# A transformer block on one Trainium2 core: input products of the feed-forward sublayers by Strassen's algorithm

## The chip, the cores and the metric

The kernel runs on 1 core of one Trainium2 chip. The metric is the time of one execution on the device in microseconds (us); a profiled execution also gives a span, from its first to its last instruction. The engines of the core are TensorE (PE; its weight loads are PEld), VectorE (DVE), ScalarE (ACT) and GpSimd (POOL); SyncE (SP) issues all transfers here.

## The reference

One block of a hybrid network on 512 tokens of width 1024, in float32: a feed-forward sublayer, a mixer (pooling and a state-space scan) and a second feed-forward sublayer, each behind a normalisation that is scaled and shifted by values computed from a conditioning vector `c`, and a last normalisation. What the change touches are the two feed-forward sublayers:

```
def swiglu(h, w_in, w_out):
    a, b = jnp.split(h @ w_in, 2, axis=-1)
    return (jax.nn.silu(a) * b) @ w_out

mod = (jax.nn.silu(c) @ w_ada[layer] + b_ada[layer]).reshape(bsz, 3, 3, D_MODEL)
h = modulate(rmsnorm(x, norm_g[layer, 0]), shift[:, 0], scale[:, 0])
x = x + 0.5 * gate[:, 0, None, :] * swiglu(h, ffn1_in[layer], ffn1_out[layer])
```

`h` is 512 x 1024, `w_in` 1024 x 5632, `w_out` 2816 x 1024.

## The kernel before, in words

**Products.** Every tile has 128 partitions. Activations are kept transposed: 8 tiles `h[k]` of 128 features by 512 tokens. A float32 value is held as two float32r numbers, a rounded high part and the difference to it, the low part; a product is three matmuls, high by high, high by low, low by high (`mm3`, lines 306 to 314), each with a weight load of its own, summed in a PSUM bank over k. A bank holds 512 columns, and there are eight.

**Pairs.** The 22 tiles of hidden features go in pairs: tile a for the gate, tile b for the value (`pair`, line 610). Each is a `product` over k = 0 to 7 of 512 columns. `glu` (line 601) takes Silu of a on ScalarE (605), multiplies by b on VectorE (607) and splits the result into parts (`split`, line 322: cast on ScalarE, difference on VectorE).

**Portions.** `ffn` (line 617) makes the pairs of one portion (PORTIONS: 8, 8 and 6), then the output products of that portion: 8 tiles m, each a product over the portion's pairs, added to `x` by `add_out` (524). In the last portion all but two output tiles are made in halves of 256 tokens, so that the next normalisation can begin. The first three pairs of the first sublayer are made in the start (`first_pairs`), k by k as the tiles `h[k]` are normalised; the first two of the second are made in halves (`in_halves`).

**Weights.** The class `Weights` (line 85) streams units of up to 8 tiles (512 KB). `load` starts the transfer into one of RAW = 3 raw tiles; `ensure` splits a unit, cast on ScalarE (123) and difference on VectorE (126), into a ring of RING = 5; `fill`, called at each new unit, keeps splits AHEAD = 3 units in front and loads RAW units in front of those.

**Conditioning.** The rest of `w_ada` (112 tiles of 256 KB, `ada_rest`, line 427) is multiplied on VectorE in the background of the first sublayer: `pump(n)` makes n steps, each a load and a `scalar_tensor_tensor` (466) on two SBUF tiles. PUMPS = (6, 1): six behind each pair, one behind each output tile. PREADA = 5 loads run ahead.

**Order.** TensorE's instructions stand in the order of the code (`manual_schedule`). In the start this holds for every engine. After it the framework orders the queues of the other engines by when inputs are ready, earlier code first; on the chip each queue is then worked in its order. Long-lived tiles come from NBIG = 50 tiles of 512 columns ("big").

Of the kernel before, what the change touches and what calls it, by code (L numbers as in the profile page):

```python
# [20 lines left out]
PORTIONS = ((0, 8), (8, 16), (16, 22))  # L21
# [10 lines left out]
RAW = 3  # L32
AHEAD = 3
NBIG = 50
NSQ = 2
NTMP = 8
PREADA = 5
PUMPS = (6, 1)
# [46 lines left out]
class Weights:  # L85


    def __init__(self, nc, pool, units, big):
        self.nc, self.pool, self.units, self.big = nc, pool, units, big
        self.raw, self.split = [], []  # L90
        self.first, self.ring = [0], [0]
        for _, count, _, extra in units:
            self.first.append(self.first[-1] + count)
            self.ring.append(self.ring[-1] + (not extra))
        self.at = self.done = 0
        self.unit = -1
        self.auto = False

    def load(self, upto):
        while len(self.raw) < min(upto, len(self.units)):  # L100
            ap, count, width, _ = self.units[len(self.raw)]
            raw = self.pool.tile([P, KD * P], F32, name="w_raw", tag="w_raw", bufs=RAW)
            self.nc.sync.dma_start(out=raw[:, :count * width], in_=ap)
            self.raw.append(raw)

    def ensure(self, upto, between=None):
        nc = self.nc
        while len(self.split) < min(upto, len(self.units)):
# [3 lines left out]
            raw, self.raw[i] = self.raw[i], None  # L112
            parts = []
            step = NT if extra else KD * P
            for c in range(0, count * width, step):
                n = min(step, count * width - c)
                if extra:
# [10 lines left out]
            self.split.append(parts)  # L128

    def fill(self, more=0):  # L130
# [7 lines left out]
        self.load(min(self.unit + AHEAD + RAW + more, len(self.split) + RAW))  # L138
# [23 lines left out]
class Norm:  # L162


    def __init__(self, blk, sub):
        self.blk, self.sub, self.rs = blk, sub, {}
        self.h = [None] * KD

# [10 lines left out]
    def apply(self, sl, k):  # L179
        if self.h[k] is None:  # L180
            self.h[k] = self.blk.new_act()
        self.blk.modulate(self.sub, k, sl, self.rs[sl], self.h, k % 2 == 1)
# [55 lines left out]
class Block:  # L238
# [26 lines left out]
    def plan(self):  # L265
# [9 lines left out]
        def ffn(f, first):  # L275
            for pi, (p0, p1) in enumerate(PORTIONS):
                for t in range(2 * max(p0, first), 2 * p1):
                    u.append((a["ffn%d_in" % f][t], KD, P, False))
# [27 lines left out]
    def mm3(self, ps, w, act, sl, first, last):  # L306
# [5 lines left out]
        T.matmul(o, lhsT=hi, rhs=ahi[:, s], start=first, stop=False)  # L312
        T.matmul(o, lhsT=hi, rhs=alo[:, s], start=False, stop=False)  # L313
        T.matmul(o, lhsT=lo, rhs=ahi[:, s], start=False, stop=last)  # L314
# [186 lines left out]
    def modulate(self, sub, k, sl, rs, h, pool):  # L501
# [7 lines left out]
        if pool:  # L509
            nc.vector.tensor_tensor(out=t, in0=self.x[:, k, s], in1=rs, op=ALU.mult)  # L510
            h32 = self.tmp()[:, :n]
            nc.scalar.activation(out=h32, in_=t, func=AF.Identity, scale=gs, bias=shift)
            self.split(h32, hi, lo, sl, pool=True)
# [62 lines left out]
    def in_halves(self, n, norm, finish):  # L576

        ws = []
        for sl in (HALF_A, HALF_B):
# [18 lines left out]
            finish(pss, sl)  # L598

# [10 lines left out]
    def pair(self, h, g):  # L610
        pa = self.bank()
        self.product(pa, None, h)
        pb = self.bank("t")
        self.product(pb, None, h)
        self.glu(pa, pb, FULL, g)

    def ffn(self, h, gs, j, gate, norm, late, spread, pumps=(0, 0)):
# [24 lines left out]
    def first_pairs(self):  # L642
# [67 lines left out]

        def prepare(k):
            self.ada_turn(k, rows[k])
            self.modulate(0, k, FULL, rs, h, False)

# [20 lines left out]
        for k in range(KD):  # L735
# [18 lines left out]
            if k > 5:  # L754
                self.W.ensure(k + 4)
        self.W.auto = True
# [8 lines left out]
        return h, gs  # L765
# [322 lines left out]
    def run(self):  # L1088
        h, gs = self.start()
# [6 lines left out]
        self.ffn(h, gs, NSTART, 2, lambda: norm(1), LATE1, SPREAD1, PUMPS)  # L1096
# [7 lines left out]
        self.in_halves(4, norms[2], glu_halves)  # L1104
        final = Final(self, 0)
        self.ffn(norms[2].h, gs, 2, 8, lambda: final, LATE2, SPREAD3)
# [80 lines left out]
```

## Time and profile before

| | |
|---|---|
| median of 3 runs | 1160.99 us (1160.63 to 1163.83) |
| the profiled execution | 1160.53 us |
| its span | 1158.5 us |
| TensorE busy | 1146.2 us, 99% |
| VectorE busy | 629.9 us, 54% |
| ScalarE busy | 396.6 us, 34% |
| GpSimd busy | 119.3 us, 10% |
| read from memory | 137.08 MB |

Matmuls are pipelined: the profile gives a duration of about 0.4 us to one whose successor starts 0.23 us later, so the price of a matmul is the distance of two starts. Busy times are unions, so they don't count an overlap twice. Stages, from the starts of the timeline: start to 69 us, first feed-forward to 400, mixer to 767, second feed-forward to the end.

### The profile page before, as it was taken

What the parts mean: (1) busy time and instruction counts of PE and PEld (TensorE: products, weight loads), DVE (VectorE), ACT (ScalarE), POOL (GpSimd) and SP (SyncE); (2) the same over time, 40 slices, a digit from 0 to 9 for tenths busy, and PEclk for the clock granted to TensorE, in tenths of its full rate; (3) what the DMA queues carried; (4) which work ended last, traced back from release to release, by engine and by line L of the source; (5) the groups of instructions that cost most, each with busy time, mean ns of one, the idle gap of its engine ahead of it and who ended that gap; (6) DMA issues with size and microseconds to landing.
All of it is one profiled execution on the core that took longest, in us unless ns stands there. A gap on an engine that the chain in (4) does not pass through costs nothing.

```text
span 1158.5 us, 15066 instructions
## 1 busy us (share of the span) xinstructions
PE 1146.2 (99%) x5948; PEld 940.8 (81%) x5948; DVE 629.9 (54%) x975; ACT 396.6 (34%) x660; POOL 119.3 (10%) x122
## 2 busy tenths in 40 slices
PE   8999999999999999999999999999999999999997
PEld 6677787777877997888888878899888888888887
DVE  4567736667363666677968595563333333333334
ACT  4352222221223453454544453343321222212232
POOL 0000000000000320023112561121000000000001
PEclk9999999999999999999999999999999999999999
DMA  9585735756352411222212213440332233323312
GB/s 346 170 293 178 261 115 198 256 190 228 123 178 91 141 60 52 77 73 73 74 55 73 73 56 91 124 131 20 91 91 91 93 103 96 92 91 91 95 33 73
DMA packets 52837, 140.17 MB, mean 121 GB/s; under 512 B 7456, under 2 KB 8864, under 8 KB 52768
## 3 DMA queue, kind: packets, MB, share of 16 engines
q1 hardware_dynamic: 52768, 139.23, 37.1%
q8 instruction: 46, 0.75, 0.3%
q14 instruction: 23, 0.19, 0.1%
HBM read 137.08 MB, written 2.10 MB: 120 GB/s over the span
## 4 chain that ended last, share of the span: by engine, by line
PE 98%; DVE 1%; DMA 0%; ACT 0%; SPq 0%; issue 0%; DVEq 0%; ACTq 0%
PE ps_mm L312 24%; PE ps_mm L313 23%; PE ps_mm L314 23%; PE ps_t L314 6%; PE ps_t L313 6%; PE ps_t L312 6%; PE ps_y L965 1%; PE ps_mm L352 1%; PE ps_mm L406 1%; PE ps_t L959 1%; PE ps_y L984 1%; PE ps_mm L375 1%; PE ps_t L927 0%; DMA x<-in_x_dram 0%; PE ps_t L930 0%; PE ps_t L932 0%
## 5 line engine op out<-in xcount | busy, mean ns | idle before, releaser
L312 PE MATMUL ps_mm<-big,w_hi 128*128 128x512 f32 (+1 forms) x1192 | 454.9, 382 | 0.0
L313 PE MATMUL ps_mm<-big,w_hi 128*128 128x512 f32 (+1 forms) x1192 | 448.1, 376 | 0.1
L314 PE MATMUL ps_mm<-big,w_lo 128*128 128x512 f32 (+1 forms) x1192 | 448.0, 376 | 0.0
L123 ACT CAST w_hi<-w_raw 128x1024 fp32r<-128x1024 f32 (+1 forms) x178 | 185.9, 1045 | 521.3 <-PE ps_mm L313 309.4
L126 DVE TENSOR_TENSOR w_lo<-w_raw,w_hi 128x1024 fp32r<-128x1024 f32 (+1 forms) x178 | 220.8, 1242 | 171.7 <-ACT w_hi L123 160.6
L312 PEld LDWEIGHTS ps_mm<-big,w_hi 128*128 128x128 f32 x1192 | 224.1, 188 | 50.3 <-issue 8.2
L314 PEld LDWEIGHTS ps_mm<-big,w_lo 128*128 128x128 f32 x1192 | 224.1, 188 | 44.8
L313 PEld LDWEIGHTS ps_mm<-big,w_hi 128*128 128x128 f32 x1192 | 224.2, 188 | 43.6 <-issue 0.7
L314 PE MATMUL ps_t<-big,w_lo 128*128 128x512 f32 x312 | 123.4, 396 | 0.0
L312 PE MATMUL ps_t<-big,w_hi 128*128 128x512 f32 x312 | 123.4, 396 | 0.0
L313 PE MATMUL ps_t<-big,w_hi 128*128 128x512 f32 x312 | 123.4, 396 | 0.0
L524 DVE SCALAR_TENSOR_TENSOR x<-ps_mm,mod,x 128x512 f32<-128x512 f32 (+1 forms) x79 | 51.1, 648 | 127.6 <-PE ps_mm L314 127.5
L331 POOL TENSOR_TENSOR sacc<-sacc,sq 128x256 f32<-128x256 f32 (+1 forms) x30 | 28.7, 956 | 747.4 <-ACT sq L386 416.1
L607 DVE TENSOR_TENSOR tmp<-tmp,ps_t 128x512 f32<-128x512 f32 x39 | 26.8, 688 | 104.4 <-PE ps_t L314 104.4
L466 DVE SCALAR_TENSOR_TENSOR big<-big,sc 128x512 f32<-128x512 f32 x98 | 73.6, 751 | 12.6 <-DMA big<-in_ada_dram 10.1
L314 PEld LDWEIGHTS ps_t<-big,w_lo 128*128 128x128 f32 x312 | 58.6, 188 | 14.2
L313 PEld LDWEIGHTS ps_t<-big,w_hi 128*128 128x128 f32 x312 | 58.6, 188 | 14.2
L312 PEld LDWEIGHTS ps_t<-big,w_hi 128*128 128x128 f32 x312 | 58.6, 188 | 14.1
L877 DVE SCALAR_TENSOR_TENSOR big<-ps_mm,vec,big 128x511 f32<-128x511 f32 (+2 forms) x60 | 44.7, 745 | 2.2 <-ACT big L875 1.3
L325 ACT CAST big<-tmp 128x512 fp32r<-128x512 f32 (+1 forms) x66 | 36.5, 556 | 2.0 <-DVE tmp L607 1.4
L312 PE MATMUL ps_mm<-big 128*128 128x256 f32 x128 | 36.5, 286 | 0.0
L313 PE MATMUL ps_mm<-big 128*128 128x256 f32 x128 | 36.2, 283 | 0.0
(179 smaller groups left out, 891.1 us busy)
## 6 DMA issues: line engine op xcount, KB each, us to landing
w_raw<-in_ffn_in_dram SPq DMA_DIRECT2D x78, 512.0 KB, 3.5
big<-in_ada_dram SPq DMA_DIRECT2D x144, 256.0 KB, 4.8
w_raw<-in_ffn_out_dram SPq DMA_DIRECT2D x44, 512.0 KB, 3.8
w_raw<-in_w_in_dram SPq DMA_DIRECT2D x32, 512.0 KB, 3.5
w_raw<-in_w_outB_dram SPq DMA_DIRECT2D x10, 512.0 KB, 3.6
w_raw<-in_w1s_dram SPq DMA_DIRECT2D x8, 384.0 KB, 5.8
w_raw<-in_w_outA_dram SPq DMA_DIRECT2D x6, 512.0 KB, 3.9
x<-in_x_dram SPq DMA_DIRECT2D x8, 256.0 KB, 5.3
```

What stands on the lines that cost most here:

```text
L123: nc.scalar.copy(out=hi[:, :n], in_=r)
L126: nc.vector.tensor_tensor(out=lo[:, :n], in0=r, in1=hi[:, :n].bitcast(F32), op=ALU.subtract)
L312: T.matmul(o, lhsT=hi, rhs=ahi[:, s], start=first, stop=False)
L313: T.matmul(o, lhsT=hi, rhs=alo[:, s], start=False, stop=False)
L314: T.matmul(o, lhsT=lo, rhs=ahi[:, s], start=False, stop=last)
L325: self.nc.scalar.copy(out=hi[:, s], in_=src[:, :n])
L331: self.nc.gpsimd.tensor_tensor(out=acc, in0=acc, in1=q, op=ALU.add)
L352: self.nc.tensor.matmul(ps[:, at + j:at + j + 1], lhsT=acc[:, c * P - c0:(c + 1) * P - c0], rhs=self.ones[:, 0:1], start=i == 0, stop=i == ...
L466: V.scalar_tensor_tensor(out=acc, in0=ws.pop(i), scalar=self.sc[:, q:q + 1], in1=acc, op0=ALU.mult, op1=ALU.add)
L524: self.nc.vector.scalar_tensor_tensor(out=xs, in0=ps[:, :n], scalar=self.mod[:, gate, m:m + 1], in1=xs, op0=ALU.mult, op1=ALU.add)
L607: nc.vector.tensor_tensor(out=g32, in0=sa, in1=pb[:, :n], op=ALU.mult)
L877: V.scalar_tensor_tensor(out=acc[:, s:], in0=ps[:, :NT - s], scalar=tap(3 - s), in1=acc[:, s:], op0=ALU.mult, op1=ALU.add)
```

## The change

Input products of pairs 3 to 21 of the first sublayer and 2 to 21 of the second are made by the Winograd form of Strassen's algorithm. A pair is seen as a 2 x 2 block product: two halves of k, two weight tiles, two halves of the tokens. `quad` makes seven block products (4 values of k, three matmuls each of 256 columns) in three banks that it writes in turns, and takes sums out of them with copies on ScalarE and additions on VectorE. `combine` makes the sums of the activations (four new pairs of tiles per sublayer for each of two sums, `tq`), in the start and in `in_halves`. The sums of weights are made on GpSimd: three of 512 columns when a pair's two tiles are loaded (`sums`), one in front of the split of the last, half, unit. A pair now has three and a half units. The low part of a pair's result goes to GpSimd but for the last pair of a portion. There are four portions (7, 5, 4, 6), four raw tiles, three conditioning loads ahead instead of five, and PUMPS = (5, 3, 3): behind a pair of the first portion, a pair of the others, an output tile.

```
-PORTIONS = ((0, 8), (8, 16), (16, 22))
+PORTIONS = ((0, 7), (7, 12), (12, 16), (16, 22))
-RAW = 3
+RAW = 4
+NSUM = 2
+LOADS = 5
-NBIG = 50
+NBIG = 51
-PREADA = 5
-PUMPS = (6, 1)
+PREADA = 3
+PUMPS = (5, 3, 3)
...
+    def sums(self, a, b):
+        G = self.nc.gpsimd
+        t = self.pool.tile([P, 2, NT], F32, name="w_sum", tag="w_sum", bufs=NSUM)
+        a11, a12, a21, a22 = a[:, :NT], a[:, NT:], b[:, :NT], b[:, NT:]
+        G.tensor_tensor(out=t[:, 0], in0=a21, in1=a22, op=ALU.add)
+        G.tensor_tensor(out=t[:, 1], in0=t[:, 0], in1=a11, op=ALU.subtract)
+        G.tensor_tensor(out=a21, in0=a11, in1=a21, op=ALU.subtract)
+        return t
...
+            elif extra == 0.5:
+                if self.rawout + 2 > RAW or self.sumout + 1 > NSUM:
+                    return
+                self.rawout += 2
+                self.sumout += 1
+                a, b = self.raw_tile(ap[0]), self.raw_tile(ap[1])
+                t = self.sums(a, b)
+                self.raw += [a, t.rearrange("p c n -> p (c n)"), b, (a[:, NT:], t[:, 1])]
...
+            if extra == 3.5:
+                raw, second = raw
+                nc.gpsimd.tensor_tensor(out=raw, in0=raw, in1=second, op=ALU.subtract)
...
-        self.load(min(self.unit + AHEAD + RAW + more, len(self.split) + RAW))
+        self.load(min(self.unit + AHEAD + LOADS + more, len(self.split) + LOADS))
...
+    def combine(self, k, src):
+        G, V = self.nc.gpsimd, self.nc.vector
+        a, b = src[k], src[k + KD // 2]
+        la, lb = slice(*HALF_A), slice(*HALF_B)
+        t, u = self.tmp(), self.tmp()
+        V.tensor_tensor(out=t[:, la], in0=a[:, lb], in1=a[:, la], op=ALU.subtract)
+        V.tensor_tensor(out=t[:, lb], in0=b[:, lb], in1=t[:, la], op=ALU.subtract)
+        G.tensor_tensor(out=u[:, la], in0=b[:, lb], in1=a[:, lb], op=ALU.subtract)
+        G.tensor_tensor(out=u[:, lb], in0=b[:, la], in1=t[:, lb], op=ALU.subtract)
+        both = self.new_act(), self.new_act()
+        self.split(t, *both[0])
+        self.split(u, *both[1])
+        return both
+
+    def quad(self, h, tq):
+        V, S, W = self.nc.vector, self.nc.scalar, self.W
+        n = KD // 2
+        low, up = h[:n], h[n:]
+        t12, t34 = [t[0] for t in tq], [t[1] for t in tq]
+        def block(ps, ws, acts, sl, first):
+            for k in range(n):
+                self.mm3(ps, ws[k], acts[k], sl, first and k == 0, k == n - 1, True)
+        x, y, z = self.bank(), self.bank("t"), self.bank("y")
+        one, two = self.tmp(), self.tmp()
+        la, lb = slice(*HALF_A), slice(*HALF_B)
+        wa = W.take(2 * n, hold=True)
+        block(x, wa[:n], low, HALF_A, True)
+        S.copy(out=one[:, la], in_=x[:, la])
+        block(y, wa[n:], up, HALF_A, True)
+        V.tensor_tensor(out=one[:, la], in0=one[:, la], in1=y[:, la], op=ALU.add)
+        W.release(2 * n, False)
+        ws = W.take(2 * n, hold=True)
+        block(x, ws[n:], t12, HALF_B, False)
+        S.copy(out=one[:, lb], in_=x[:, la])
+        block(z, ws[:n], t12, HALF_A, True)
+        S.copy(out=two[:, lb], in_=z[:, la])
+        W.release(2 * n, False)
+        wb = W.take(2 * n, hold=True)
+        block(x, wb[:n], t34, HALF_A, False)
+        V.tensor_tensor(out=two[:, lb], in0=two[:, lb], in1=x[:, la], op=ALU.add)
+        block(z, W.take(n, hold=True), up, HALF_B, False)
+        V.tensor_tensor(out=one[:, lb], in0=one[:, lb], in1=z[:, la], op=ALU.add)
+        block(x, wb[n:], t34, HALF_B, False)
+        W.release(3 * n)
+        return one, two, x
+
+    def quad_pair(self, h, tq, g, pool):
+        V, S = self.nc.vector, self.nc.scalar
+        one, two, x = self.quad(h, tq)
+        la, lb = slice(*HALF_A), slice(*HALF_B)
+        S.activation(out=one, in_=one, func=AF.Silu)
+        V.tensor_tensor(out=two[:, lb], in0=one[:, lb], in1=two[:, lb], op=ALU.mult)
+        V.tensor_tensor(out=two[:, la], in0=one[:, la], in1=x[:, la], op=ALU.mult)
+        self.split(two, *g, pool=pool)
...
-                self.pair(h, gs[i])
-                self.pump(pumps[0])
+                self.quad_pair(h, tq, gs[i], i < p1 - 1)
+                self.pump(pumps[pi > 0])
+            if not pi:
+                self.pump(1)
+                self.pump(1)
...
-                self.pump(pumps[1])
+                self.pump(pumps[2])
...
+        def whole(k):
+            sums[k] = self.big()
+            nc.gpsimd.tensor_tensor(out=sums[k], in0=h[k][0].bitcast(F32), in1=h[k][1].bitcast(F32), op=ALU.add)
+            if k >= KD // 2:
+                tq.append(self.combine(k - KD // 2, sums))
```

In the second sublayer the normalised tile is also kept whole (`modulate` writes it to a tile of its own before the split, for every k), and `combine` runs after the first half of `in_halves`. `skip_group_check` in `mm3` and a smaller scratch area for transfers are the rest.

## Rows read from the trace of the kernel before

**Rows 1.** The page: busy time by engine; the chain that ended last

```profile
PE 1146.2 (99%) x5948; PEld 940.8 (81%) x5948; DVE 629.9 (54%) x975; ACT 396.6 (34%) x660; POOL 119.3 (10%) x122
...
PE 98%; DVE 1%; DMA 0%; ACT 0%; SPq 0%; issue 0%; DVEq 0%; ACTq 0%
```

**Rows 2.** Stretches (from:to): length, busy us (instructions) by engine, clock, DMA

```profile
core 0: us, PE busy (x) PEld busy (x) DVE busy (x) ACT busy (x) POOL busy (x), PEclk, DMA share, GB/s
0.00:69.48 69.48, 64.21 (x390) 47.91 (x391) 37.26 (x78) 29.81 (x49) 2.80 (x6) 0.98 0.74 255
...
172.50:259.70 87.20, 87.20 (x409) 68.00 (x407) 55.15 (x72) 24.78 (x36) 0.00 (x0) 1.00 0.61 210
...
752.60:767.00 14.40, 14.40 (x124) 14.40 (x122) 4.47 (x8) 3.90 (x6) 3.20 (x3) 1.00 0.37 128
...
917.26:1001.26 84.00, 84.00 (x361) 67.62 (x360) 27.42 (x29) 23.63 (x30) 0.00 (x0) 1.00 0.32 94
```

**Rows 3.** Timeline of TensorE, 512 columns: start, duration (us), line

```profile
150.09 0.40 PE L312 MATMUL ps_mm<-big,w_hi 128*128 128x512 f32 x1
...
157.09 0.40 PE L312 MATMUL ps_mm<-big,w_hi 128*128 128x512 f32 x1
```

**Rows 4.** Timeline of TensorE, 256 columns, 120 matmuls from first to last

```profile
752.59 0.28 PE L312 MATMUL ps_mm<-big,w_hi 128*128 128x256 f32 x1
...
766.67 0.28 PE L314 MATMUL ps_mm<-big,w_lo 128*128 128x256 f32 x1
```

**Rows 5.** Groups by line and shape, second feed-forward: count, busy us, mean ns

```profile
L126 DVE TENSOR_TENSOR w_lo<-w_raw,w_hi 128x1024 fp32r<-128x1024 f32 x56 | 68.6, 1225 | 82.8 <-ACT w_hi L123 78.3
...
L123 ACT CAST w_hi<-w_raw 128x1024 fp32r<-128x1024 f32 x57 | 60.1, 1055 | 233.9 <-PE ps_mm L313 148.5 <-issue 64.9 <-PE ps_t L313 16.2
...
L607 DVE TENSOR_TENSOR tmp<-tmp,ps_t 128x512 f32<-128x512 f32 x20 | 13.8, 689 | 71.2 <-PE ps_t L314 71.2
L327 DVE TENSOR_TENSOR big<-tmp,big 128x512 fp32r<-128x512 f32 x20 | 13.7, 685 | 0.0
...
L325 ACT CAST big<-tmp 128x512 fp32r<-128x512 f32 x20 | 12.5, 623 | 0.0
...
L327 DVE TENSOR_TENSOR big<-tmp,big 128x256 fp32r<-128x256 f32 x2 | 0.8, 426 | 0.1
L607 DVE TENSOR_TENSOR tmp<-tmp,ps_mm 128x256 f32<-128x256 f32 x2 | 0.8, 421 | 6.6 <-PE ps_mm L314 6.6
```

**Rows 6.** Groups of ScalarE by shape: a 256-column copy out of PSUM

```profile
L409 ACT COPY tmp<-ps_mm 128x256 f32<-128x256 f32 x8 | 3.0, 374 | 16.1 <-PE ps_mm L406 16.1
```

**Rows 7.** Line 987, GpSimd, two 512-column inputs: minimum, median, maximum ns

```profile
L987 POOL TENSOR_TENSOR big<-big x12: 1270/1298/2141, 493.0 to 696.5; 128x512 f32<-128x512 f32 x12
```

**Rows 8.** Groups of VectorE by shape: a conditioning step

```profile
L466 DVE SCALAR_TENSOR_TENSOR big<-big,sc 128x512 f32<-128x512 f32 x98 | 73.6, 751 | 12.6 <-DMA big<-in_ada_dram 10.1
```

**Rows 9.** Timeline of VectorE in the mixer

```profile
573.64 2.27 DVE L126 TENSOR_TENSOR w_lo<-w_raw,w_hi 128x1024 fp32r<-128x1024 f32 x1 [1.03 <-PE ps_t L961]
...
576.12 0.73 DVE L974 SCALAR_TENSOR_TENSOR big<-big,vec,ps_y 128x512 f32<-128x512 f32 x1
...
581.59 1.22 DVE L126 TENSOR_TENSOR w_lo<-w_raw,w_hi 128x1024 fp32r<-128x1024 f32 x1
...
664.08 1.01 DVE L342 TENSOR_TENSOR root<-root 128x4 f32<-128x4 f32 x1
```

**Rows 10.** Timeline of GpSimd at the same moments

```profile
573.55 1.27 POOL L987 TENSOR_TENSOR big<-big 128x512 f32<-128x512 f32 x1
...
576.02 1.33 POOL L331 TENSOR_TENSOR big<-big,sq 128x512 f32<-128x512 f32 x1
581.75 1.93 POOL L331 TENSOR_TENSOR big<-big,tmp 128x384 f32<-128x384 f32 x1 [4.40 <-DVE tmp L985]
...
664.04 1.04 POOL L778 TENSOR_TENSOR tmp<-tmp 128x510 f32<-128x510 f32 x1
```

**Rows 11.** The page, DMA issues: the conditioning loads

```profile
big<-in_ada_dram SPq DMA_DIRECT2D x144, 256.0 KB, 4.8
```

More of the change, by code (lines that the diff above doesn't have):

```diff
@@ L93, in __init__ @@
             self.first.append(self.first[-1] + count)
-            self.ring.append(self.ring[-1] + (not extra))
+            self.ring.append(self.ring[-1] + (extra is not True))
         self.at = self.done = 0
@@ L167, in __init__ @@
         self.h = [None] * KD
+        self.whole = [None] * KD
     def scale(self, k):
@@ L181, in apply, with combine @@
             self.h[k] = self.blk.new_act()
-        self.blk.modulate(self.sub, k, sl, self.rs[sl], self.h, k % 2 == 1)
+            if self.sub == 2:
+                self.whole[k] = self.blk.big()
+        self.blk.modulate(self.sub, k, sl, self.rs[sl], self.h, k % 2 == 1, self.whole[k])
+    def combine(self):
+        return [self.blk.combine(k, self.whole) for k in range(KD // 2)]
 class Final(Norm):
@@ L275, in ffn @@
         def ffn(f, first):
+            w = a["ffn%d_in" % f]
             for pi, (p0, p1) in enumerate(PORTIONS):
-                for t in range(2 * max(p0, first), 2 * p1):
-                    u.append((a["ffn%d_in" % f][t], KD, P, False))
+                for j in range(max(p0, first), p1):
+                    u.append(((w[2 * j], w[2 * j + 1]), KD, P, 0.5))
+                    u.extend((None, n, P, part) for n, part in ((KD, 1.5), (KD, 2.5), (KD // 2, 3.5)))
                 stream(a["ffn%d_out%d" % (f, pi)])
@@ L303, in mixer_order, with mm3 @@
                 + [("outB", m) for m in range(MLATE)])
-    def mm3(self, ps, w, act, sl, first, last):
+    def mm3(self, ps, w, act, sl, first, last, again=False):
         hi, lo = w
@@ L311, in mm3 @@
         T = self.nc.tensor
-        T.matmul(o, lhsT=hi, rhs=ahi[:, s], start=first, stop=False)
-        T.matmul(o, lhsT=hi, rhs=alo[:, s], start=False, stop=False)
-        T.matmul(o, lhsT=lo, rhs=ahi[:, s], start=False, stop=last)
+        T.matmul(o, lhsT=hi, rhs=ahi[:, s], start=first, stop=False, skip_group_check=again)
+        T.matmul(o, lhsT=hi, rhs=alo[:, s], start=False, stop=False, skip_group_check=again)
+        T.matmul(o, lhsT=lo, rhs=ahi[:, s], start=False, stop=last, skip_group_check=again)
     def product(self, ps, ws, acts, sl=FULL, mid=None):
@@ L498, in pump, with modulate @@
             next(self.bg, None)
-    def modulate(self, sub, k, sl, rs, h, pool):
+    def modulate(self, sub, k, sl, rs, h, pool, whole=None):
         nc = self.nc
@@ L598, in in_halves @@
             finish(pss, sl)
+            if sl == HALF_A and norm.sub == 2:
+                tq = norm.combine()
+        return tq
     def glu(self, pa, pb, sl, g):
@@ L608, in glu, with ffn @@
         self.split(g32, g[0], g[1], sl)
[L610 to L617, printed above, removed]
+    def ffn(self, h, tq, gs, j, gate, norm, late, spread, pumps=(0, 0, 0)):
         for pi, (p0, p1) in enumerate(PORTIONS):
@@ L713, in prepare @@
             self.modulate(0, k, FULL, rs, h, False)
+            if k > 1:
+                whole(k - 2)
         for k in range(3):
@@ L755, in first_pairs @@
                 self.W.ensure(k + 4)
+                whole(k)
         self.W.auto = True
@@ L1088, in run @@
     def run(self):
-        h, gs = self.start()
+        h, tq, gs = self.start()
         norms = {}
```

43 lines of the change are left out of this document (28 added, 15 removed).

## The prediction

> **What bounds the kernel now.** I read the page first: TensorE is busy 99% of the span and the chain that ended last is TensorE for 98%, so the sum of matmul times is the time [rows 1]. The table of stretches comes next. Over eight pairs of the first feed-forward TensorE never stops, VectorE works 55.2 of 87.2 us, GpSimd not at all; over 84 us of the second, VectorE works 27.4 [rows 2]. Third, the timeline of TensorE, since a busy matmul is no price: starts give it. From 150.09 to 157.09 us there are 30 steps of 512 columns, 0.2333 us each [rows 3]; from 752.59 to 766.67 us 119 steps of 256 columns, each with its own weight load, 0.1183 us each [rows 4]. Half the columns cost 0.507 of the time, though the weight loads are then busy for the whole stretch [rows 2]. That decides whether Strassen can pay at all.
>
> **What is removed.** The changed pairs are 3 to 21 of the first feed-forward and 2 to 21 of the second, 39. A pair is 2 x 8 x 3 = 48 matmuls of 512 columns, 48 x 0.2333 = 11.20 us [rows 3]. A quad is 7 blocks x 4 x 3 = 84 matmuls of 256, 84 x 0.1183 = 9.94 us [rows 4]. The gain is 1.26 us a pair, 49 us in all, if TensorE never waits.
>
> A rule speaks against this. The Trainium skill, TensorE: Matmul & The Clock Gate, section Back-to-back issue gap, gives a sustained stream with weight loads about 81 ns a matmul at 128 columns and 131 at 512; an estimate between them, 98 ns at 256, would make a quad 8.2 us against 6.3 for a pair, 31% longer instead of 11% shorter. The two timelines here show 118 and 233 ns, so I take the trace.
>
> **What is added, per quad.** Durations are from [rows 5] unless named.
> - VectorE: 3.5 units of weights instead of 2, three differences of 1.225 (line 126) and one of 512 columns, priced by the 512-column difference of line 327 (0.685): 4.36. Three adds and a multiply that read PSUM, 4 x 0.421 = 1.68. One multiply from two SBUF tiles, 0.43. Together 6.47 us; before it was 2 x 1.225 + 0.689 + 0.685 = 3.82.
> - ScalarE: 3 x 1.055 + 0.62 for weights, three copies of 0.374 [rows 6], Silu and cast of about 0.62 each: 6.2 of 9.94 us. It fits; what is behind a late cast waits with it.
> - GpSimd: three weight sums at loading, one subtraction before the last half unit, and the low part of the product (not for the last pair of a portion): 5 x 1.298 = 6.5 us [rows 7].
> - DMA: 1 MB a pair as before. Conditioning steps: 3 behind each pair instead of 6 (5 in the first portion), 3 instead of 1 behind each output tile, 0.751 us each [rows 8].
>
> **GpSimd and VectorE stand in each other's way.** At 664.04 us GpSimd starts an operation of 1.04 us; a VectorE operation of 4 columns, both inputs in SBUF, starts 0.04 later and takes 1.01, ending with it. A weight difference that starts during a GpSimd operation of 1.27 takes 2.27 instead of 1.225. The other way, GpSimd takes 1.93 for 384 columns behind a difference that ends 1.06 us after its start. But a VectorE operation that reads PSUM takes 0.73 right through a GpSimd operation [rows 9, 10]. So VectorE with two SBUF inputs and GpSimd take turns; weight differences and conditioning steps are such operations. In [rows 9, 10] the difference ended 1.09 us after GpSimd did, 0.13 less than its own 1.225: a collision costs VectorE 1.30 - 0.13 = 1.17, five of them 5.85 us a pair. How many collide, no row of a quad shows. Ends: none, VectorE at 6.5 and TensorE at 9.94; all, VectorE at 12.3.
>
> Without conditioning VectorE has 3.5 of 9.94 us free and reads PSUM for 1.7, so about half of the GpSimd operations should meet no rival: 6.47 + 2.9 = 9.4, still under TensorE. What remains are short waits: the same PSUM bank is written again 12 matmuls (1.42 us) after it must be emptied, once by VectorE and three times by ScalarE. An add of 0.42 behind a difference of 1.225, or of 2.27 if that collided, is 0.2 to 1.3 us late, and most are not: I take 0.35 a pair, quads at **10.3 us**.
>
> With 3 conditioning steps VectorE needs 6.47 + 2.25 = 8.72 and is hardly ever free; I let 60% collide (3.5): **12.2 us**, with 5 steps 6.47 + 3.76 + 3.5 = **13.7**. The steps run out at 22 + 24 + 15 + 24 + 12 + 15 = 112, in the third portion's output, so the fourth portion has none.
>
> **The sum.** First feed-forward:
> - portion of four quads: 4 x 13.7, less 3.8 for the pump behind the last one, which falls into the output stage, 51.0 against 44.8, +6.2;
> - next nine: 9 x 12.2 = 109.8, less 2 x 2.25 for the same, less 2 x 4.2 for sums of the first two pairs made during the output stage before (six operations at 60% of 1.17), 96.9 against 100.8, -3.9;
> - last six at 10.3, -5.4.
>
> Second feed-forward: 20 x 0.9 = -18. Together -21.
>
> What is split ahead at the two ends of a portion cancels, three units either way; only the sums move out of it.
>
> What is late next:
> - Start. The last activation sums need GpSimd 1.3, VectorE 0.85, cast 0.62, difference 0.69, behind three weight units (3.7) and the combination before (2.2 on VectorE, 2.6 on GpSimd), 12 us; from the last normalised tile to its first use are 18 x 0.2333 + 33 x 0.1183 = 8.1. So +4 (0 to 8).
> - Second feed-forward. Four combinations of 2.2 on VectorE and 1.3 on GpSimd, 14, and 3.7 of weights before 120 x 0.1183 = 14.2 us have passed: +3.5 (0 to 9).
> - Portion ends. The last product needs 0.42 + 0.62 + 0.69, 4.0 with one operation ahead on each of two engines; a portion of four gives 2.3 us, of five 3.0. At half the time: 0.9 and 0.5, twice, +3.
> - Eight more output additions each are 0.75 us on VectorE beside TensorE's output stage: nothing, with three units of 5.6 us split ahead; uncovered, 12 us.
>
> -21 + 10.5 = -10.5. The profiled execution took 1160.53 us, so 1150.0; the median of the runs shown is 0.46 above it, the difference I neglect.
>
> **Rivals.**
> 1. *The two engines miss each other.* For it: the sums are made at loading, and units are split three ahead, some 60 matmuls or 7 us before use, so both engines have room to step aside. All quads near 10.05: 39 x 1.15 = -45, half the late items +5: 1121.
> 2. *The shared turn becomes the bound,* slower. Per quad GpSimd's 6.5 and VectorE's two-input 4.8, with 2.25 of conditioning, are 13.5 us of turns before what overlaps. The place is the weight differences of the first feed-forward; it decides from about 80% collisions. At 90% (5.27 a quad): the first portion 4 x 15.5 - 3.8 = 58.2, +13; the next nine 9 x 14.0 - 4.5 - 2 x 6.3 = 109, +8; the other 26 quads 26 x 11.74, less 6.3 for each of four portions whose first sums are made in an output stage, 280 against 291, -11. With the late items 1160.5 + 10 + 10.5 = 1181. Against it: VectorE reads PSUM for 1.7 us a pair.
> 3. *Conditioning loads.* Only four are under way instead of six, landing in 4.8 us [rows 11], and the trace has 10 us of waits on them already [rows 8]. The fifth step of a pump would wait 4.8 - 3 x 0.75 = 2.5 us at the head of VectorE's queue, four times: 1150 + 10 = 1160, no change.
> 4. *The weight loads set the pace,* and a narrow matmul costs nearly what a wide one does: at the bound of 0.2333, 84 x 0.2333 - 11.20 = 8.4 us more a quad, 1160 + 328 + 10 = 1498, slower. [Rows 4], taken with a new load for each matmul, exclude it but for 0.01. The Trainium skill, TensorE: Matmul & The Clock Gate, section Back-to-back issue gap, would by the estimate above give 1306. That the change makes fewer or more products than it says is excluded by the code: 84 matmuls a quad.
>
> **How the numbers follow.** Forecast 0.43, own range 1136 to 1157; rival 1 0.23; rival 2 0.22; rival 3 0.11; rival 4 0.01. A measurement here tells 0.3%, 3.5 us, from no change. Faster: 0.43 + 0.23 = 0.66; same: 0.11; slower: 0.23. The range takes in rivals 1 and 3 and rival 2 up to its price: 1119 to 1182.
>
> **What would show it.** Quads of 10.3 us in the second feed-forward and 12 to 14 in the first, with TensorE's idle time ended by VectorE adds and ScalarE copies; weight differences with a mean well above 1.225 and GpSimd above 1.3; output stages unchanged at 0.2333 a matmul. Quads of 10 us everywhere would mean that collisions are rare; quads over 11.2 in the second feed-forward make me wrong on the sign; waits on conditioning loads or on weight loads mean rival 3.

## The result, and the profile after

The changed kernel takes 1212.73 us (1207.93 to 1216.59) against 1161.85 for the kernel before on the same chip: ratio 1.0434, interval 1.0391 to 1.0478. It is slower by 51 us; I had forecast 1150 and a range that ends at 1182. The profiled execution took 1214.54, its span is 1212.8, 54.3 more than before.

The page, busy time by engine and the chain that ended last, to set against [rows 1]:

```profile
PE 1136.5 (94%) x7352; PEld 999.4 (82%) x7352; DVE 839.6 (69%) x1226; ACT 514.1 (42%) x879; POOL 447.2 (37%) x333
...
PE 69%; DVE 5%; issue 2%; ACT 1%; DMA 1%; SPq 0%; DVEq 0%
```

TensorE has less to do than before (1136.5 us, was 1146.2) and a longer span to do it in. The view of waits on TensorE says for whom it stopped (line and tile that waited <- engine, tile and line waited for: us in total, times, longest):

```profile
PE ps_mm L359 <- ACT tmp L402: 19.9, 2, 17.3
PE ps_mm L359 <- DVE tmp L414: 18.0, 9, 4.0
PE ps_y L594 <- DVE big L574: 9.1, 4, 3.1
PE ps_mm L360 <- DVE big L435: 7.2, 5, 2.4
```

All its waits add up to 69 us; before they were 5.2. Line 402 is the first copy out of a quad, 414 an addition in it, 594 the matmuls that finish a conditioning row, 574 a conditioning step, 435 a difference.

By stage (lengths taken from the starts of matmuls in both traces; a pair before took 219.2 us / 19 = 11.54 in the first sublayer, matmuls of the conditioning rows included):

| stage | before, us | after, us | difference |
|---|---|---|---|
| until the first changed pair begins | 63.9 | 72.1 | +8.2 |
| FFN1, its four quads of the first portion | 46.2 | 71.7 | +25.6 |
| FFN1, the next nine | 103.8 | 111.5 | +7.6 |
| FFN1, the last six | 69.2 | 61.4 | -7.8 |
| FFN1, output products of 16 pairs | 90.9 | 116.5 | +25.6 |
| mixer, with the last output stage before it and the two pairs in halves behind it | 425.6 | 428.2 | +2.5 |
| FFN2, quads and their output stages | 313.6 | 306.2 | -7.4 |

The table of stretches shows the same (from:to, length, busy us and instructions of PE, PEld, DVE, ACT, POOL, granted clock, DMA): first portion, its output stage, second portion, last portion of FFN1, then a full portion of FFN2 and its short output stage before the last portion.

```profile
72.09:143.82 71.73, 48.02 (x353) 45.92 (x353) 58.80 (x69) 31.38 (x49) 30.75 (x20) 0.81 0.41 136
143.82:190.51 46.69, 42.64 (x196) 33.08 (x193) 38.04 (x50) 8.45 (x13) 11.11 (x7) 0.96 0.73 235
190.51:255.34 64.83, 55.70 (x437) 53.06 (x435) 54.47 (x64) 29.95 (x46) 28.58 (x17) 0.95 0.47 154
...
371.79:433.21 61.42, 61.41 (x505) 60.10 (x504) 43.77 (x53) 34.62 (x53) 32.01 (x19) 1.00 0.33 105
...
955.93:1006.84 50.91, 50.91 (x422) 50.05 (x421) 36.52 (x44) 28.77 (x44) 28.42 (x17) 1.00 0.36 109
...
1076.96:1106.12 29.16, 25.63 (x98) 20.00 (x97) 14.53 (x15) 4.57 (x6) 10.33 (x8) 0.88 0.21 67
```

Where conditioning is over, TensorE is busy for the whole stretch at clock 1.00 and a quad takes 61.42 / 6 = 10.24 and 50.91 / 5 = 10.18 us: the forecast of 10.3 holds there, and the gain is real. Where conditioning, combinations or a start run beside them, VectorE is busy for 82 to 84% of the stretches above and TensorE waits, and then its clock falls too.

**The first quad** takes 32.8 us. Two entries of TensorE's timeline, with the idle time in front of them and what ended it:

```profile
74.50 0.39 PE L361 MATMUL ps_mm<-big,w_lo 128*128 128x256 f32 x1 [1.91 <-DVE w_lo L160]
96.05 0.58 PE L359 MATMUL ps_mm<-big,w_hi 128*128 128x256 f32 x1 [17.27 <-ACT tmp L402]
```

ScalarE's timeline just before 96.05:

```profile
86.70 0.62 ACT L433 CAST big<-tmp 128x512 fp32r<-128x512 f32 x1 [1.10 <-POOL tmp L379]
87.22 0.59 ACT L716 ACTIVATE tmp<-ps_mm 128x512 f32<-128x512 f32 x1
91.72 0.62 ACT L433 CAST big<-tmp 128x512 fp32r<-128x512 f32 x1 [3.90 <-DVE tmp L718]
...
95.14 0.59 ACT L716 ACTIVATE tmp<-ps_mm 128x512 f32<-128x512 f32 x1
95.63 0.36 ACT L402 COPY tmp<-ps_mm 128x256 f32<-128x256 f32 x1
```

The copy that empties the quad's first bank stands at the end of ScalarE's queue, behind the casts of the last combinations and behind Silu and cast of the first three pairs, and each of these casts waits for VectorE or GpSimd. Those two are at each other's heels in these 20 us, and again and again one of them takes nearly twice its own time (1.225 us for the difference, 1.30 for GpSimd's operation). VectorE's timeline:

```profile
72.15 2.29 DVE L160 TENSOR_TENSOR w_lo<-w_raw,w_hi 128x1024 fp32r<-128x1024 f32 x1
74.37 2.31 DVE L160 TENSOR_TENSOR w_lo<-w_sum,w_hi 128x1024 fp32r<-128x1024 f32 x1
```

GpSimd's, at the same moments:

```profile
73.32 2.27 POOL L822 TENSOR_TENSOR big<-big 128x512 f32<-128x512 f32 x1
75.55 2.26 POOL L146 TENSOR_TENSOR w_raw<-w_raw,w_sum 128x512 f32<-128x512 f32 x1
```

**A late addition.** TensorE stops for 3.8 us in the second portion:

```profile
217.80 0.39 PE L359 MATMUL ps_mm<-big,w_hi 128*128 128x256 f32 x1 [3.83 <-DVE tmp L414]
```

VectorE's queue before it:

```profile
209.82 2.31 DVE L160 TENSOR_TENSOR w_lo<-w_sum,w_hi 128x1024 fp32r<-128x1024 f32 x1
212.05 4.23 DVE L574 SCALAR_TENSOR_TENSOR big<-big,sc 128x512 f32<-128x512 f32 x3
216.20 1.22 DVE L160 TENSOR_TENSOR w_lo<-w_raw,w_hi 128x1024 fp32r<-128x1024 f32 x1
217.33 0.41 DVE L414 TENSOR_TENSOR tmp<-tmp,ps_mm 128x256 f32<-128x256 f32 x1
```

The product that line 414 reads ends at 212.3, but the addition starts 5 us later: three conditioning steps stand in front of it, each at nearly twice its own 0.751 us [rows 8], and a difference.

**The conditioning rows.** In the output stages TensorE stops at line 594, in front of everything that stands behind it in its queue:

```profile
155.16 0.42 PE L594 MATMUL ps_y<-big,ones 128*32 128x128 f32 x8 [1.28 <-DVE mod L549]
183.60 0.43 PE L594 MATMUL ps_y<-big,ones 128*32 128x128 f32 x8 [2.77 <-DVE big L574]
266.40 0.48 PE L594 MATMUL ps_y<-big,ones 128*32 128x128 f32 x8 [3.14 <-DVE big L574]
```

**The clock.** The mean granted clock is 0.969, before 0.996. Of the two levels, 2.4 and 1.2 GHz, that makes 2 x 0.031 x 1212.8 = 75 us at the lower one against 2 x 0.004 x 1158.5 = 9. The busy time times the missing share of the clock, added up stretch by stretch, is some 29 us lost at half clock (before 4.5). The third quad, from 120.46, has no wait at all and takes 11.93 us at clock 0.88, behind a quad with a wait of 4.0 us; its first matmuls (lines 359, 360 and 361 in turn, with the same weights and shapes) start 0.214 us apart, 12 of them in 2.57 us, and later ones 0.118:

```profile
120.45 0.41 PE L359 MATMUL ps_mm<-big,w_hi 128*128 128x256 f32 x1
...
123.02 0.41 PE L359 MATMUL ps_t<-big,w_hi 128*128 128x256 f32 x1
```

So the 54 us come together as 64 us more idle time and 25 more at half clock, less 19 x 1.3 + 20 x 0.95 = 44 of quads that are shorter at full clock (10.25 against 11.54 and 11.2); 9 us remain for effects I did not separate, such as conditioning rows that now fall into output stages.

### The profile page after: what moved, and what is told of

Same layout as the page of the kernel before. It is cut to its first block, busy times and chain, and to the rows that moved or that the text cites. A ratio compares the mean times of both kernels' runs of the same rounds, so it can differ in the third digit from the quotient of the medians.

```text
span 1212.8 us, 18828 instructions
## 1 busy us (share of the span) xinstructions
PE 1136.5 (94%) x7352; PEld 999.4 (82%) x7352; DVE 839.6 (69%) x1226; ACT 514.1 (42%) x879; POOL 447.2 (37%) x333
## 4 chain that ended last, share of the span: by engine, by line
PE 69%; DVE 5%; issue 2%; ACT 1%; DMA 1%; SPq 0%; DVEq 0%
PE ps_mm L359 18%; PE ps_mm L360 18%; PE ps_mm L361 18%; PE ps_y L359 2%; PE ps_y L360 2%; PE ps_y L361 2%; DVE w_lo L160 1%; PE ps_t L359 1%; PE ps_t L360 1%; PE ps_y L1083 1%; PE ps_t L361 1%; DVE big L574 1%; DMA big<-in_ada_dram 1%; DVE big L435 1%; PE ps_mm L460 1%
## 5 line engine op out<-in xcount | busy, mean ns | idle before, releaser
L359 PE MATMUL ps_mm<-big,w_hi 128*128 128x256 f32 (+1 forms) x1504 | 517.1, 344 | 41.0 <-ACT tmp L402 19.9
L360 PE MATMUL ps_mm<-big,w_hi 128*128 128x256 f32 (+1 forms) x1504 | 508.3, 338 | 6.8 <-DVE big L435 5.5
L361 PE MATMUL ps_mm<-big,w_lo 128*128 128x256 f32 (+1 forms) x1504 | 507.7, 338 | 1.9 <-DVE w_lo L160 1.9
L359 PEld LDWEIGHTS ps_mm<-big,w_hi 128*128 128x128 f32 x1504 | 289.0, 192 | 83.5 <-ACT tmp L402 20.4
L160 DVE TENSOR_TENSOR w_lo<-w_raw,w_hi 128x1024 fp32r<-128x1024 f32 (+2 forms) x217 | 270.6, 1247 | 120.1 <-ACT w_hi L157 115.4
L157 ACT CAST w_hi<-w_raw 128x1024 fp32r<-128x1024 f32 (+2 forms) x217 | 209.5, 967 | 306.8 <-PE ps_mm L360 183.9
L360 PEld LDWEIGHTS ps_mm<-big,w_hi 128*128 128x128 f32 x1504 | 289.7, 193 | 38.5 <-DVE big L435 7.0
L115 POOL TENSOR_TENSOR w_sum<-w_raw 128x512 f32<-128x512 f32 x39 | 66.5, 1706 | 172.8 <-DMA w_raw<-in_ffn_in_dram 147.9
L359 PE MATMUL ps_y<-big,w_hi 128*128 128x256 f32 x312 | 92.1, 295 | 0.1
L360 PE MATMUL ps_y<-big,w_hi 128*128 128x256 f32 x312 | 88.1, 282 | 0.0
L361 PE MATMUL ps_y<-big,w_lo 128*128 128x256 f32 x312 | 87.9, 282 | 0.0
L160 DVE TENSOR_TENSOR w_lo<-w_sum,w_hi 128x1024 fp32r<-128x1024 f32 x39 | 71.0, 1820 | 20.1 <-ACT w_hi L157 20.0
L116 POOL TENSOR_TENSOR w_sum<-w_sum,w_raw 128x512 f32<-128x512 f32 x39 | 68.2, 1750 | 2.8
```

Of the source, the lines that this page charges most:

```text
L115: G.tensor_tensor(out=t[:, 0], in0=a21, in1=a22, op=ALU.add)
L116: G.tensor_tensor(out=t[:, 1], in0=t[:, 0], in1=a11, op=ALU.subtract)
L157: nc.scalar.copy(out=hi[:, :n], in_=r)
L160: nc.vector.tensor_tensor(out=lo[:, :n], in0=r, in1=hi[:, :n].bitcast(F32), op=ALU.subtract)
L359: T.matmul(o, lhsT=hi, rhs=ahi[:, s], start=first, stop=False, skip_group_check=again)
L360: T.matmul(o, lhsT=hi, rhs=alo[:, s], start=False, stop=False, skip_group_check=again)
```

## The experiments

In the expectations theory 1 is the shared turn of VectorE and GpSimd, theory 4 the first quad's place behind the work of the start, theory 6 TensorE's clock behind a wait. The diffs are against the changed kernel.

**No weight sums.** The four GpSimd operations a quad on weights are left out, so the products are made with other weights.

```
-                t = self.sums(a, b)
-                self.raw += [a, t.rearrange("p c n -> p (c n)"), b, (a[:, NT:], t[:, 1])]
+                self.raw += [a, b, b, a[:, NT:]]
...
-            if extra == 3.5:
-                raw, second = raw
-                nc.gpsimd.tensor_tensor(out=raw, in0=raw, in1=second, op=ALU.subtract)
```

> Leaves out the four weight sums per quad on GpSimd (the products are made from unsummed tiles); everything else as in the changed kernel (1212.7 us). Theory 1, VectorE is overloaded in the first feed-forward by two things added together, the turns with GpSimd and the conditioning steps: without sums the weight differences return to a mean of 1.25 us or less (1.25 to 1.82 by group now), waits of TensorE on the VectorE addition in quads fall from 15.6 us to under 5, the first quad's wait from 17 to about 10, and the clock loss with them: 1170 to 1185 us. Rival 2, the conditioning steps alone are to blame: the waits in the quads keep more than 10 us, 1200 us or more. Rival 3, the turns alone are to blame: the waits in quads and on conditioning rows all go, 1140 to 1155 us.

1166.86 us, ratio 1.0037 (1.0021 to 1.0052), 46 us less than the change, between theory 1's range and the other one. The mean of a weight difference falls to 1250 ns and waits for the adds from 18.0 to 6.7 us, less far than the under 5 expected. But 13.0 us of wait for the first copy stay (about 10 expected), and 8.0 for conditioning rows. So the sums, by the turns and the work together, are the largest single part, but without them the change would still not be faster than before.

**Fewer conditioning steps.** Six of eight steps of each conditioning sum do no arithmetic (their loads stay); the sums miss those terms.

```
-            else:
+            elif q == KD - 1:
```

> Leaves out six of the eight conditioning steps of each sum (loads stay, arithmetic of steps 1 to 6 goes, 84 of 112 steps). Theory 1: VectorE gets back 63 us or more in the first feed-forward; waits on the VectorE addition there fall from 15.6 us to under 5, waits on conditioning rows (10.1 us) go, the first quad's 17 us stay, since no conditioning step stands before it: 1175 to 1188 us. Rival 3, turns alone: the waits on additions keep more than 10 us, 1200 us or more.

1186.91 us, ratio 1.0214 (1.0162 to 1.0265), 26 us less, as theory 1 has it. The waits, with the same lines as above:

```profile
PE ps_mm L359 <- ACT tmp L402: 20.2, 3, 17.2
PE ps_mm L360 <- DVE big L435: 8.5, 5, 2.5
PE ps_y L594 <- DVE big L574: 5.4, 3, 2.8
...
PE ps_mm L359 <- DVE tmp L414: 2.5, 4, 1.1
```

The waits for adds all but go, and the one in the first quad is untouched, as expected; of the waits for rows, which I expected to go, 5.4 us stay. Neither cause hides the other.

**Pairs in the first portion.** Pairs 3 to 6 of the first sublayer as before the change; the sums of the activations are still made.

```
+PAIRS = {1: 7, 2: 2}
...
+                if i < PAIRS[1 if gate == 2 else 2]:
+                    self.pair(h, gs[i])
+                else:
+                    self.quad_pair(h, tq, gs[i], i < p1 - 1)
```

> Pairs 3 to 6 of the first feed-forward are made as before, as pairs of 96 half-width equivalents, and quads begin with the second portion; the activation sums stay in the start. Theory 4, the first quad waits because its emptying stands on ScalarE behind all work of the start, which the activation sums on VectorE and GpSimd stretch: that portion takes 46 to 50 us instead of 71.7, 1188 to 1194 us. Rival: the work of the start is only moved and stalls the first pairs as long, through banks that the start has not emptied: 1205 us or more.

1183.06 us, ratio 1.0181 (1.0140 to 1.0221), 30 us less, beyond what I expected. The portion takes 46.3 us again, the wait of 17.3 us is gone, and adds cost 12.8. The four quads of this portion, meant to gain, cost as much as the three output stages.

**Conditioning rows later.** The matmuls of line 594 are put six steps later, so that VectorE has finished.

```
-            if turn and self.pumps > turn[1]:
+            if turn and (self.pumps > turn[1] if turn[0][0] == 2 else q == KD - 2):
```

> The conditioning rows' matmuls stand six conditioning steps behind the last step of their sum in TensorE's queue, instead of behind the next pump (not for the first vector, which is needed early). Theory 5, output stages of the first feed-forward are 7, 7 and 12 us over their matmuls because these four matmuls wait at the head of TensorE's queue for VectorE and the clock falls afterwards: waits on them fall from 10.1 us to under 2, the three stages from 116.5 us to 95 to 102, the time to 1193 to 1203 us. Rival: VectorE is simply behind, and the wait moves to additions and weight differences: no change beyond 4 us, 1208 to 1217 us.

1207.59 us, ratio 1.0392 (1.0341 to 1.0443): 5 us less by the medians, with intervals that overlap. Waits at line 594 fall from 10.4 to 5.0 us and the three output stages from 116.5 to 105.1, but waits for adds rise to 21.3 and for copies to 21.3. VectorE is late as such; most of the wait moves.

**TensorE kept busy.** 70 matmuls whose result is overwritten stand where TensorE waited in the first quad.

```
+FILLERS = 70
...
         block(x, wa[:n], low, HALF_A, True)
         S.copy(out=one[:, la], in_=x[:, la])
+        if not self.pumps and not self.filled:
+            self.filled = True
+            for _ in range(FILLERS):
+                self.nc.tensor.matmul(y, lhsT=wa[0][0], rhs=low[0][0], start=True, stop=True, skip_group_check=True)
         block(y, wa[n:], up, HALF_A, True)
```

> Adds 70 matmuls of 512 columns, whose sums are thrown away, between the first and the second block of the first quad, so that TensorE works while it would wait for ScalarE's first copy. The queues of the other engines are unchanged. Theory 6, a wait costs again through the clock: the granted clock of the first quad rises from 0.69 to 0.9 or more, the third quad, which has no wait of its own and took 11.93 us at 0.88, takes 10.1 to 10.6, the second falls from 15.6 to about 14, the time by 3 to 6 us to 1207 to 1210. Rival: the low clock comes from something else (the narrow matmuls themselves): the third quad stays at 11.5 or more and the time within 3 us of 1212.7 or above.

1207.15 us, ratio 1.0386 (1.0356 to 1.0415). The first quad has 2.8 us idle instead of 19.9 (0.7 us in front of its first matmul counted) and clock 1.00 instead of 0.69, and takes 29.05 us. The second, expected at about 14 us, still takes 15.5, with its own wait of 3.9. The third quad is busy throughout in both kernels. Its stretch in the changed kernel:

```profile
120.46:132.39 11.93, 11.93 (x94) 11.39 (x93) 9.81 (x14) 6.05 (x10) 2.54 (x2) 0.88 0.46 157
```

With the first quad's wait filled:

```profile
114.67:125.70 11.03, 11.03 (x94) 10.49 (x93) 9.82 (x14) 5.93 (x10) 2.57 (x2) 0.96 0.51 166
```
 By the medians work that computes nothing gains 5.6 us, but the two ratios' intervals overlap; what shows the clock's share is the third quad, which does the same work without a wait in either kernel, behind a wait of about 4 us in both, and is 0.9 us shorter. It misses the 10.1 to 10.6 expected as well as the rival's 11.5: half clock behind the wait of 4 us still comes, but lasts 3.5 us instead of 5.5.

**Weight sums on VectorE.** The same four operations, on the other engine.

```
-        G = self.nc.gpsimd
+        G = self.nc.vector
...
-                nc.gpsimd.tensor_tensor(out=raw, in0=raw, in1=second, op=ALU.subtract)
+                nc.vector.tensor_tensor(out=raw, in0=raw, in1=second, op=ALU.subtract)
```

> The four weight sums of a quad are made on VectorE instead of GpSimd, which keeps the low part of the product and its share of the activation sums. VectorE gets 4 x 0.685 = 2.7 us more to do a quad, and four of five GpSimd operations that it can collide with are gone. Theory 1 in its sharper form (a collision costs VectorE 1.17, its own sum 0.69): weight differences fall to a mean of 1.3 us or less, 1190 to 1205 us; quads of the second feed-forward stay at 10.1 to 10.6, VectorE then has 9.8 of 10.1 us to do. Rival, GpSimd takes real work off VectorE and collisions are the smaller part: 1213 to 1235 us, and quads of the second feed-forward rise over 10.6.

1193.41 us, ratio 1.0267 (1.0247 to 1.0288): 19 us faster than with the sums on GpSimd. VectorE's groups by shape (count, busy us, mean ns), in the changed kernel:

```profile
L160 DVE TENSOR_TENSOR w_lo<-w_raw,w_hi 128x1024 fp32r<-128x1024 f32 x170 | 225.2, 1325 | 98.4 <-ACT w_hi L157 93.9 <-PE ps_t L1079 2.7 <-DMA big<-in_ada_dram 0.9
...
L160 DVE TENSOR_TENSOR w_lo<-w_sum,w_hi 128x1024 fp32r<-128x1024 f32 x39 | 71.0, 1820 | 20.1 <-ACT w_hi L157 20.0
```

And with the sums on VectorE:

```profile
L160 DVE TENSOR_TENSOR w_lo<-w_raw,w_hi 128x1024 fp32r<-128x1024 f32 x170 | 213.3, 1255 | 91.5 <-ACT w_hi L157 88.1 <-PE ps_t L1079 2.7
L160 DVE TENSOR_TENSOR w_lo<-w_sum,w_hi 128x1024 fp32r<-128x1024 f32 x39 | 47.4, 1215 | 6.7 <-ACT w_hi L157 6.7
```

A difference of a summed tile goes from 1820 ns to 1215, its undisturbed time [rows 5]. The page's busy times of this run:

```profile
PE 1128.6 (95%) x7352; PEld 993.0 (83%) x7352; DVE 874.0 (73%) x1382; ACT 513.9 (43%) x879; POOL 200.5 (17%) x177
```

The time is in the range, but not for the reason given. VectorE is busy 34 us longer than in the changed kernel: its 156 sums take 128.5 us, 0.82 each, and the operations that had taken turns with them get back 69, 0.44 a sum. So the sums on GpSimd did not cost VectorE more than they saved it. Its waiters are served sooner all the same: TensorE's waits for adds fall from 18.0 to 10.1 us and the first copy's from 17.3 to 12.6. Moving the sums to the idle engine slowed the kernel. Whether by GpSimd's own lateness, which the sums pass on to the weights, or by the long differences that stand in front of additions, is not shown. Quads of the second sublayer stay at 10.1 to 10.6 us but for two (13.0 and 11.2).

**Strassen in the second sublayer alone.** The first sublayer with pairs, portions (8, 8, 6) and conditioning (6 steps a pair, 1 an output tile, 5 ahead) as before the change; in the second, quads for pairs 3 to 21 with portions (8, 8, 6).

```
-PORTIONS = ((0, 7), (7, 12), (12, 16), (16, 22))
+PAIRS = {1: 22, 2: 3}
+PORTIONS = {1: ((0, 8), (8, 16), (16, 22)), 2: ((0, 8), (8, 16), (16, 22))}
...
-PREADA = 3
-PUMPS = (5, 3, 3)
+PREADA = 5
+PUMPS = (6, 6, 1)
...
```

> The first feed-forward is undone (pairs, portions, conditioning and loads ahead as before, no activation sums in the start); the second has quads for tiles 3 to 21, tile 2 as a pair, and the portions of before (8, 8, 6). Theory: everything lost is lost in the first feed-forward and at the edges of the second; 19 quads at 10.2 against 11.2 give 19 us, the combination 2 to 4 us back, no stage of four: 1143 to 1151 us, faster than before by 1 to 1.6%. Rival: what the quads give the stages around them take back also here: 1157 us or more.

1152.52 us, ratio 0.9908 (0.9886 to 0.9930): 0.9% faster than the kernel before, with the whole interval below 1, though 1.5 us above what I expected. No quad waits; all take 10.08 to 10.43 us. All waits of this kernel above 1.2 us:

```profile
PE ps_mm L364 <- POOL big L439: 3.3, 1, 3.3
PE ps_mm L464 <- DVE big L804: 2.8, 1, 2.8
PE ps_mm L867 <- ACT big L857: 2.0, 1, 2.0
```

The first stands at 784.0, in the two pairs made in halves behind the mixer (line 439 here is the low part of a normalised tile on GpSimd), and nearly 10 us of half clock follow it; the other two stand in the first 23 us of the kernel. Its weight differences of summed tiles have a mean of 1963 ns, worse than in the changed kernel: the two engines collide at least as often, and no quad waits.

**One more plain pair in the second sublayer**, so that the first weight sums miss the normalisation; against the run before this:

```
-PAIRS = {1: 22, 2: 3}
+PAIRS = {1: 22, 2: 4}
```

> The kernel of the second-sublayer run, with one more plain pair in front of its quads (quads 4 to 21). That run's trace has its one long half-clock stretch (10.2 us) behind a wait of 3.33 us of TensorE for GpSimd's low part of a normalised tile, which stood behind five weight sums in GpSimd's queue. Theory: with the first sums two units later they miss the normalisation; 3.3 us of wait and 4 to 5 us of half clock go, a quad's 1.1 us is given up: 1145 to 1148. Rival: the stretch is the combination's own or the sums only collide a little later: 1152 to 1155.

1152.71 us, ratio 0.9916 (0.9902 to 0.9931), the rival. The wait for GpSimd falls to 1.0 us, and one of 3.8 for the same line's operation on VectorE takes its place.

**The last portion of the first sublayer as well** (conditioning 8 steps a pair, 5 in the second portion, 3 an output tile, 3 loads ahead; the combinations are made behind the first four pairs of the second portion); against the second-sublayer run:

```
-PAIRS = {1: 22, 2: 3}
-PORTIONS = {1: ((0, 8), (8, 16), (16, 22)), 2: ((0, 8), (8, 16), (16, 22))}
+PAIRS = {1: 16, 2: 3}
+PORTIONS = {1: ((0, 10), (10, 16), (16, 22)), 2: ((0, 8), (8, 16), (16, 22))}
-PREADA = 5
-PUMPS = (6, 6, 1)
+PREADA = 3
+PUMPS = (8, 5, 3)
...
+                if gate == 2 and pi == 1 and len(tq) < KD // 2:
...
+                    tq.append(self.combine(kk, sums))
```

> The kernel of the second-sublayer run (1152.5 us), with the last six pairs of the first sublayer made by Strassen again, the activation sums made during the second of three portions (10, 6 and 6 pairs) and the conditioning steps pulled forward (8, 5 and 3). Theory: a quad gains wherever VectorE has no conditioning beside it, so six quads of 10.1 to 10.5 us instead of 11.2 give 4 to 6.5 us, less 1 to 3 for the first of them: 1147 to 1151. Rival: the loss in the first sublayer is the sublayer's own (combinations, conditioning and weight sums crowd wherever they stand): waits move to the second portion or its output, 1153 to 1165.

1160.42 us, ratio 0.9983 (0.9973 to 0.9993). Its six quads take 10.1 to 10.5 us but for the first (10.8), as the theory says, but TensorE waits 9.0 us at the conditioning rows: the rival.

**Both edits together:** the last-portion run with a plain pair more in the second sublayer.

```
-PAIRS = {1: 16, 2: 3}
+PAIRS = {1: 16, 2: 4}
```

> Both edits together. If both theories hold their gains add: 1139 to 1146. If only one does, it stands near that one's own time.

1161.64 us, ratio 0.9990 (0.9980 to 1.0000), no gain over either.

**Conditioning steps earlier**, against the last-portion run:

```
-PUMPS = (8, 5, 3)
+PUMPS = (8, 6, 1)
```

> The kernel of the last-portion run (1160.4 us), whose six quads take 10.1 to 10.8 us with almost no wait while TensorE waits 9.0 us for conditioning rows in its output stages: conditioning steps 8 behind a pair of the first portion, 6 behind one of the second, 1 behind an output tile (there 8, 5 and 3). Theory: the six quads do gain, and the loss is the three steps behind an output tile; with one there the rows arrive in time, some 9 us of waits and 3 of half clock go: 1147 to 1151, faster than the second-sublayer run. Rival: VectorE has no room for the steps in the second portion either, beside the combinations and three splits ahead: the waits move there, 1155 to 1162.

1156.99 us, ratio 0.9965 (0.9951 to 0.9979), inside the rival's range. It is 3.4 us better by the medians than with three steps an output tile, and 2 by the ratios, whose intervals overlap a little; but waits at the rows fall only to 7.2 us, and two of the six quads now wait for adds, 1.7 us. The steps need VectorE wherever they stand; the version with quads in the second sublayer alone remains the best.

## Why the prediction was wrong

- **The price of a quad was right.** 9.94 us by [rows 4], 10.3 forecast with small waits; undisturbed quads take 10.1 to 10.5. The prediction's estimate from the figures of the Trainium skill, TensorE: Matmul & The Clock Gate, section Back-to-back issue gap, would have made a quad longer than a pair; 0.118 us a matmul in the trace decides. Rival 4 is out. Rival 3 is out as an addition: VectorE's waits for conditioning loads are 9.5 us in all, 10.1 before, and none of TensorE's large waits ends with a load. But 6.7 of the 9.5 now fall into output stages, in front of steps that rows wait for.
- **The turns were there, and priced too high.** In the last portion of the first sublayer VectorE's operations lose about 1.4 us a quad to them (5 x 0.69 on summed tiles, 5 x 0.41 on half units, 14 x 0.04 on raw ones, 5 x 0.2 on the multiply, by five), half of the 2.9 forecast, and GpSimd's 2.3; in the first portion VectorE's lose 2.6 of 3.5 forecast. The additions that read PSUM keep 0.41 to 0.42 us everywhere. What failed is the step from load to time. Rival 2 named the right engines, slower, at 1181, by saturation; but VectorE is busy 84% of the second portion and TensorE still waits there. VectorE's queue is worked in its order, and the forecast's only price for a late add, 0.2 to 1.3 us, has it stand behind one difference; beside conditioning it stands behind three steps too, and is 5 us late (217.33 above).
- **"Start: +4 (0 to 8)" failed.** Measured: +8.2 before the first quad, and that quad takes 32.8 us, 19.1 over its forecast 13.7. I counted the last activation sum's way to its first use, and not what the quad's first copy stands behind on ScalarE: casts that wait for combinations, and Silu and cast of three pairs. The run with pairs in the first portion gives 30 us back.
- **"Output stages unchanged at 0.2333 a matmul" failed.** The output stages of the first sublayer take 25.6 us more, where I had "nothing" for the additions and about 1.5 for portion ends. Of it 13.3 us are idle time, 10.4 of them in front of rows, about 3 are the matmuls of seven rows more, and most of the remaining 9 are half clock. With three conditioning steps behind each tile instead of one, VectorE is late; the matmuls of a finished row stand in TensorE's queue and pass that on. I priced the steps as VectorE's load, and never asked who waits for the step. No run alone restores the stages: from 116.5 us they fall to 105.1 with the rows later, 107.5 without most of the conditioning arithmetic and 105.9 without weight sums, against 90.9 before. So the steps are only a part of it; how the rest divides is not shown.
- **The clock was in no term.** Some 25 us more than before are lost at half clock behind waits (29 less 4.5). That a wait filled with work shortens a later quad that does not wait shows the mechanism; the 25 us are worked out from the granted clock, not tried as a whole.
- **The second sublayer** gained 7.4 us and cost 2.5 in the mixer; I had -18 + 3.5 + half of the portion ends. Its first quad takes 14.5 us, 4.2 over the forecast (2.67 of it a wait for the same first copy, clock 0.88). The output stage of the portion of four takes 29.2 us instead of 96 x 0.2333 = 22.4: 2.19 and 1.33 us of wait for the last product's split, and half clock behind them; I had 0.9.
- **Quads beside conditioning came near their price by luck.** The three later quads of the first portion take 39.0 us against 3 x 13.7 = 41.1, the next nine 111.5 against 9 x 12.2 = 109.8. These prices were VectorE's load, with VectorE hardly ever idle; but it is busy 11.0 us a quad in the first case and 10.9 and 10.2 in the two portions of the second, and TensorE's waits and clock make up the rest. And the 3.8 and 4.5 us for pumps and 8.4 for sums that fall into output stages, which I took off, did not come: that work did not shorten the portions, and the output stages became longer.
- **The sign.** Stage by stage, measured against forecast: start +8.2 (+4), first portion +25.6 (+6.2), next nine +7.6 (-3.9), last six -7.8 (-5.4), output stages of the first sublayer +25.6 (+1.5), mixer +2.5 (+3.5), quads of the second sublayer -15.8 (-18), its output stages +8.4 (+1.5): +54.3 against -10.6. The first quad (19.1), the output stages of the first sublayer (24.1) and the next nine, whose credits did not come (11.5), make 55 of the 65 us between them and turn a gain into a loss.

One reading of the rows is off, without touching the sum: the stretches of 87.2 and 84 us that the prediction calls eight pairs begin at the second tile of a pair [rows 2] and hold seven and a half, and the first pair behind the start begins at 63.9 us, not 69.

What stays open: how the 46 us of the sums divide between turns and GpSimd's own lateness (the run with the sums on VectorE shows only that VectorE's busy time is not what they cost), what else makes the output stages longer, and the last few microseconds by which the parts do not add up (their gains overlap).

## What to carry to other kernels

Where an engine is the bound, price an added operation by what stands behind it in its queue and who waits for that, not by the engine's busy share. Put work of this kind where nothing else runs beside it: 19 quads behind the mixer gain some 10 us, and 39 with conditioning, normalisation and combinations beside half of them lose 51. Moving an operation to an idle engine can lose even where it takes load off the busy one: here it took turns with it, and what waited for either came later.

## What the runs showed that I had not expected

- The kernel is faster with the weight sums on the busier engine, VectorE: 1193.4 against 1212.7 us for the same arithmetic, although VectorE is then busy 874.0 us instead of 839.6.
- A wait of 4.0 us is followed by matmuls 0.214 us apart instead of 0.118, and the next quad, without a wait, takes 1.7 us more (11.93 against 10.2). With an earlier wait, of 17.3 us, filled by matmuls that compute nothing, it takes 11.0, though the wait of 4 us is still there.
- Collisions alone need cost no time: in the fastest version differences of summed tiles take 1963 ns instead of 1225, and no quad waits.
